# A mixed mLSTM and attention block: both groups of transposes directly behind each block of scores

## The chip, the cores and the metric

The kernel runs on one core of a Trainium2 chip. The metric is the device time of one execution in microseconds (us). Of the kernel before there are three timed runs (median 1693.31 us) and one execution under the hardware profiler.

## What is computed

One layer with two branches over a sequence of 1024 tokens and a width of 1024, all in float32. Cut to what matters here:

```
h = rmsnorm(x)
proj = h @ w_in                       # 12 segments: q, k, v, o, z, gates of branch a; q, k, v, z of branch b; two gates
branch a: mLSTM in both directions over 4 heads of 256 (chunked recurrence), rmsnorm, times sigmoid(o) * silu(z)
branch b: for each of 8 heads of 128:
    dq, dk = rope(q), rope(k)                            # two halves j of 64
    p = softmax(dq_0 dk_0 / 8) - lam * softmax(dq_1 dk_1 / 8)
    y_b = rmsnorm(p @ v) * silu(z)
mix = sigmoid(g_a) * (y_a @ w_branch_a) + sigmoid(g_b) * (y_b @ w_branch_b)
out = rmsnorm(x + mix @ w_out)
```

## The kernel before

Each product in float32 is made of three matmuls on halves: an operand is split into a high part H (rounded) and a low part L (the rest), and HH + HL + LH is summed in PSUM. Names that end in H and L are these parts.

The program runs in stages: an opening and a stage of projections with fewer products (to about 480 us), the attention (branch b, to about 1140 us), the mLSTM (branch a, to about 1400 us), then the mixing and the output. `build` writes down **units**, small pieces of work of TensorE with all that other engines do for them, in one list. On TensorE the order of that list is kept; on VectorE (DVE), ScalarE (ACT) and GpSimd (POOL) the framework's scheduler sets an order of its own, fixed at build time, and each engine takes its instructions strictly in that order. SyncE (SP) issues the DMAs.

In the attention the list is made by a planner, `Weaver`. It keeps a clock of its own, and `weave` merges the attention's own units with filling work (projections for the next head, products with v's weights, gate projections): it always takes the unit that is ready first. When a unit is ready follows from the table `LAG` (how long after another unit, and how long a PSUM bank is held) and from the number of banks.

The units of a head h, with t the block of 128 queries:
- S (`scores`): 12 matmuls on 64 rows each into two tiles S of 128x1024, which take four of the eight PSUM banks. VectorE finds the maximum (nm, L1066), ScalarE the exponential (e, L1068), VectorE the weighted difference of both (L1074).
- T (`transposes`), two groups of four transposes of e. Each group takes one of the two T banks; ScalarE copies it to pH (L1087), VectorE makes pL (L1088), and then the bank is free.
- PV (`pv`): 24 products with v for two blocks, in one T bank; ScalarE copies the result to att (L1101).
- M (`squares`): two transposes of att in a T bank, which ScalarE squares and sums (L1111). After the last pair GpSimd makes the scale rs from it (rb_v, rb_y, L146 to L152, L1118).
- G (`scale`): four transposes of rs in a T bank; VectorE multiplies it into zg (L1131).

The filling work uses the other two banks, pj. `da_proj` makes q and k of the next head: two projections (L552, "rope weights"), which VectorE multiplies by cos and sin (m, hl, L984 to L996); GpSimd rotates and splits them in six operations (L997 to L1001), and eight DMAs bring them to kst and qq (L1006). The tile hl exists once. `da_v` makes v for two heads (L574; ScalarE vH, VectorE vL L1043). `fill(n)` takes n gate projections; the tuple `FILL` says how many each head gets.

The mLSTM begins with loads of keys, values and gate rows (k, v, gb, HL in `ml_units`). Its keys are transposed and weighted (kwH by ScalarE, L1216), while W is made of gb by GpSimd (L1271) and ScalarE (L1273).

Of the kernel before, what the change touches and what calls it, by code (L numbers as in the profile page):

```python
# [8 lines left out]
F32R = mybir.dt.float32r  # L9
# [5 lines left out]
S = 1024  # L15
# [13 lines left out]
def two_pi_parts():  # L29
# [5 lines left out]


INF = 1.0e9
FILL = (0, 0, 0, 0, 0, 0, 0, 1)
Z_EARLY = (0, 1, 3, 5)
MM = 0.214  # L40
TP = 0.109

LAG = dict(Th=2.2, Sh=5.0, PVh=3.7, Mh=8.1, qk=14.0, T=6.8, PV=3.7, M=4.5, F=6.0, TTh=1.9, TT=3.2, POh=1.6,
           PO=1.7, Wh=0.3, W=2.0, STh=2.1, ST=4.9, th=1.8, t=4.1, aq=9.0, outh=6.6, out=14.0, G=6.0)


class Unit:
# [5 lines left out]
    def __init__(self, cost, fn, keys=(), tag=None, hold=0.0, name=None, after=(), lane=0):  # L53
        self.cost, self.fn, self.keys = cost, fn, keys
        self.tag, self.hold, self.name, self.after, self.lane = tag, hold, name, after, lane


def wide(t):

    return t.rearrange("p k e -> p (k e)").rearrange("p (k e) -> p k e", e=256)  # L60


class Weaver:
# [2 lines left out]
    def __init__(self):  # L66
        self.now, self.free, self.ends, self.banks, self.out, self.coming = 0.0, {}, {}, {}, [], set()

    def ready(self, u):
        t = 0.0  # L70
        for n, d in u.after:
            t = max(t, self.ends.get(n, INF if n in self.coming else 0.0) + d)
        if u.tag:
            held = sorted(self.free.get(u.tag, []))
            n = self.banks.get(u.tag, 1)
            if len(held) >= n:
                t = max(t, held[-n])
        return t

    def put(self, u):  # L80
        self.now = max(self.now, self.ready(u)) + u.cost
        if u.tag:
            self.free[u.tag] = (self.free.get(u.tag, []) + [self.now + u.hold])[-8:]
        if u.name:
            self.ends[u.name] = self.now
        self.out.append(u)
# [5 lines left out]
    def weave(self, *lists):  # L92


        lanes = {}
        for i, un in enumerate(lists):
            total, c = sum(u.cost for u in un) or 1.0, 0.0
            for u in un:
                lanes.setdefault((i, u.lane), []).append((c / total, u))
                c += u.cost  # L100
        self.coming = {u.name for un in lists for u in un if u.name}
        heads = list(lanes.values())
        while heads:
            best = min(heads, key=lambda l: (max(self.ready(l[0][1]), self.now), l[0][0]))
            u = best.pop(0)[1]
            self.put(u)
            self.coming.discard(u.name)
            heads = [l for l in heads if l]


class Block:
# [862 lines left out]
    def da_proj(self, h, st):  # L974
        A, v, a, p, q = self.A, self.v, self.a, self.p, self.q
        w1 = self.w1
        fb = lambda x: x.bitcast(F32)
        kA, kB = ("rope", h, 0), ("rope", h, 1)

        def first(half, pa):  # L980
            c = slice(half * 512, (half + 1) * 512)
            m = [w1.tile([128, 512], F32, name=f"m{i}", tag=f"m{i}", bufs=1) for i in range(2)]
            st["m"] = m
            v.tensor_tensor(out=m[0], in0=pa, in1=self.cosT[:, c], op=ALU.mult)  # L984
            v.tensor_tensor(out=m[1], in0=pa, in1=self.sinT[:, c], op=ALU.mult)

        def second(half, pb):
            c = slice(half * 512, (half + 1) * 512)
            if half == 0:
                st["k"] = w1.tile([128, 2, S], F32R, name="kst", tag="kst", bufs=2)  # L990
            qq = st["q", half] = w1.tile([128, 2, 512], F32R, name="qq", tag="qq", bufs=3)
            m = st["m"]

            hl = w1.tile([128, 4, 512], F32R, name="hl", tag="hl", bufs=1)
            v.tensor_tensor(out=fb(hl[:, 2]), in0=pb, in1=self.sinT[:, c], op=ALU.mult)
            v.tensor_tensor(out=fb(hl[:, 3]), in0=pb, in1=self.cosT[:, c], op=ALU.mult)  # L996
            p.tensor_tensor(out=m[0], in0=m[0], in1=fb(hl[:, 2]), op=ALU.subtract)  # L997
            p.tensor_tensor(out=m[1], in0=fb(hl[:, 3]), in1=m[1], op=ALU.add)
            for i in range(2):
                p.tensor_copy(hl[:, i, :], m[i])  # L1000
                p.tensor_tensor(out=hl[:, 2 + i, :], in0=m[i], in1=fb(hl[:, i, :]), op=ALU.subtract)  # L1001
            for x in range(2):
                for i, to in enumerate((st["k"][:, :, c], qq)):
                    for j in range(2):
                        r, g = 64 * j + 32 * x, 64 * (1 - i) + 32 * j
                        q.dma_start(out=fb(to[r:r + 32]), in_=fb(hl[g:g + 32, x::2]))  # L1006

        kz = ("w_in", OFF["bz"] + 128 * h)

        def zz(half, ps):  # L1010
            st["g", half] = g = w1.tile([128, 512], F32, name="zg", tag="zg", bufs=2)
            a.activation(out=g, in_=ps, func=AF.Tanh, scale=0.5)
            v.scalar_tensor_tensor(out=g, in0=g, scalar=1.0, in1=ps, op0=ALU.add, op1=ALU.mult)

        qk = []
        for half in range(2):
            qk += self.proj(kA, half, lambda ps, half=half: first(half, ps))
            qk += self.proj(kB, half, lambda ps, half=half: second(half, ps), name=("qk", h))
        def load(half):
            t = w1.tile([128, 512], F32, name="zr", tag="zr", bufs=2)  # L1020
            q.dma_start(out=t, in_=self.zd[h][:, half * 512:(half + 1) * 512])
            zz(half, t)

        if h in Z_EARLY:
            z = [Unit(0.0, lambda half=half: load(half), name=("z", h) if half else None) for half in range(2)]
        else:
            z = self.proj(kz, 0, lambda ps: zz(0, ps)) + self.proj(kz, 1, lambda ps: zz(1, ps), name=("z", h))
        for half in range(2):
            z[(half + 1) * len(z) // 2 - 1].after = ((("G", h - 1, half), LAG["G"]),)
        return qk, z  # L1030

    def da_v(self, n, sts):

        a, v, w1 = self.a, self.v, self.w1

        def done(s2, ps):
            for i, st in enumerate(sts):
                if s2 == 0:
                    st["v"] = tuple(w1.tile([128, 8, 128], F32R, name=f"v{x}", tag=f"v{x}", bufs=3) for x in "HL")
                vH, vL = (x[:, 2 * s2:2 * s2 + 2, :] for x in st["v"])  # L1040
                src = ps[:, :, 128 * i:128 * i + 128]
                a.copy(vH, src)
                v.tensor_tensor(out=vL, in0=src, in1=vH.bitcast(F32), op=ALU.subtract)  # L1043
        return self.v_units("bv", n, done, ((("PV", 2 * n - 2, 3, 1), 0.0),))

    def da_parts(self, h, st):
        v, a, p, q, w1 = self.v, self.a, self.p, self.q, self.w1
# [76 lines left out]
        def scale(half):  # L1124
# [3 lines left out]
            for i in range(4):  # L1128
# [6 lines left out]
            S=lambda t: Unit(6 * MM, lambda: scores(t), tag="S", hold=LAG["Sh"], name=("S", h, t), after=((("qk", h), LAG["qk"]),)),  # L1135
            T=lambda t, g: Unit(4 * TP, lambda: transposes(t, g), tag="T", hold=LAG["Th"], name=("T", h, t, g),
                                after=((("S", h, t), LAG["T"]),)),
            PV=lambda t2, g: Unit(12 * TP, lambda: pv(t2, g), tag="T" if g == 0 else None, hold=LAG["PVh"], name=("PV", h, t2, g),
                                  after=((("T", h, 2 * t2 + 1, g), LAG["PV"]),)),
            M=lambda t2: Unit(2 * TP, lambda: squares(t2), tag="T", hold=LAG["Mh"], name=("M", h, t2),  # L1140
                              after=((("PV", h, t2, 1), LAG["M"]), (("z", h if t2 == 3 else -1), 0.0))),
            G=lambda half: Unit(4 * TP, lambda: scale(half), tag="T", hold=LAG["Th"], name=("G", h, half),
# [2 lines left out]
    @staticmethod  # L1145
    def da_cycle(cur, prev, t):

        before = cur if t > 0 else prev
        un = []
        if cur:  # L1150
            un.append(cur["S"](t))
        own = cur if t >= 4 else prev
        if own and t % 2 == 0:
            un.append(own["M"]((t // 2 - 2) % 4))
        if prev and t in (4, 5):
            un.append(prev["G"](t - 4))
        own = cur if t >= 3 else prev
        pair = ((t - 1) // 2 - 1) % 4
        if own and t % 2 == 1:
            un += [own["PV"](pair, 0), own["PV"](pair, 1)]  # L1160
        if before:
            un.append(before["T"]((t - 1) % 8, 0))
        if before:
            un.append(before["T"]((t - 1) % 8, 1))
        return un


# [206 lines left out]
    def ml_units(self, heads, gates):  # L1374
# [4 lines left out]
        x, un = heads[0], []  # L1379
        take = lambda n: [gates.pop(0) for _ in range(n)]  # L1380
        hl = lambda x, c: x["gb"](c) + x["HL"](c)
        un += x["k"](3) + x["gb"](0) + x["v"](3) + x["k"](2) + x["v"](2) + x["k"](1) + x["HL"](0) + x["v"](1)
        un += take(8) + x["weigh"](3, 1) + take(3) + x["state"](3, 1) + x["k"](0) + x["v"](0)
        un += x["weigh"](2, 1) + take(5) + x["state"](2, 1) + hl(x, 1)
        un += x["weigh"](1, 1) + take(4) + x["state"](1, 1) + x["split"](0)
# [177 lines left out]
    def build(self):  # L1563
# [21 lines left out]
        with pool(name="const", bufs=1) as self.const, \  # L1585
# [99 lines left out]
            w.banks.update(S=1, T=2)  # L1685
            qk, z = zip(*[self.da_proj(h, sts[h]) for h in range(NH_B)])
            v0 = self.da_v(0, sts[0:2])
            w.add(do(lambda: setattr(self, "ahead", True)), *fill(1), *qk[0], *z[0], *v0[:20])
            prev = None
            for h in range(NH_B):  # L1690
                cur = self.da_parts(h, sts[h])
# [90 lines left out]
```

## Time and profile before

| | us |
|---|---|
| three runs | 1692.19, 1693.31, 1695.94 |
| the profiled execution | 1692.5 |
| its span, first to last instruction | 1690.7 |
| TensorE busy | 1640.5 |
| VectorE busy | 1019.6 |
| ScalarE busy | 774.9 |
| GpSimd busy | 660.4 |
| mean granted clock of TensorE | 0.995 |

The profiled execution lies 0.8 us under the median of the runs. In the lines below, PE is TensorE's matmuls and PEld its weight loads. "L552" is a line of the kernel, "pj<-hH,wH" says what is written from what, and "[2.15 <-DVE hl L996]" that the engine stood idle for 2.15 us, until VectorE's instruction of line 996 was done. Matmuls overlap, so on TensorE the distance from start to start tells what one costs, not its duration. A row of the waits reads: who waited, for whom, us in total, times, the longest.

### The profile page before, as it was taken

The page shows a single profiled execution, that of the slowest core. Times are in us where ns is not written, and L with a number is a line of the kernel's source. Part 1 is how long each engine was busy: PE and PEld are TensorE (multiplying, and loading weights), DVE is VectorE, ACT ScalarE, POOL GpSimd, SP SyncE. Part 2 cuts the span into 40 slices and gives each one's busy share as a digit, 9 for nine tenths or more (in the row PEclk, how much of TensorE's full clock was granted, in tenths as well). Part 3 has the DMA queues.
Part 4 walks back from the last instruction along what each step waited for, and adds up shares of the span by engine and source line. Part 5 has one row for each costly group of instructions (what it writes and reads, how often), then busy time and mean ns, then how long its engine had stood idle before and what let it go on. Part 6 is the DMA issues. An engine that isn't in the chain of part 4 may idle for free. (4 is left out here: it accounts for less than half of the span.)

```text
span 1690.7 us, 25288 instructions
## 1 busy us (share of the span) xinstructions
PE 1640.5 (97%) x9335; PEld 1377.7 (81%) x9335; DVE 1019.6 (60%) x1817; ACT 774.9 (46%) x1548; POOL 660.4 (39%) x713
## 2 busy tenths in 40 slices
PE   7999999999999999999999999999999999999998
PEld 5898778878778779788887977788988877888887
DVE  5634876787743876777676677713666664245533
ACT  6433555555532545544544555524566654022221
POOL 5754676666644343425154343222232222212000
PEclk9999999999999999999999999999999999999999
DMA  5433434443443132223132122028877527443222
GB/s 180 148 125 127 140 113 143 120 137 112 125 149 88 51 75 68 53 68 88 38 88 51 44 76 63 32 88 270 264 203 216 165 82 273 145 167 100 75 94 81
DMA packets 189710, 199.75 MB, mean 118 GB/s; under 512 B 11929, under 2 KB 143346, under 8 KB 189586
## 3 DMA queue, kind: packets, MB, share of 16 engines
q1 hardware_dynamic: 188386, 196.03, 38.3%
q10 hardware_dynamic: 1200, 2.11, 0.3%
q8 instruction: 73, 1.20, 0.3%
q14 instruction: 51, 0.42, 0.1%
HBM read 124.60 MB, written 56.72 MB: 107 GB/s over the span
## 5 line engine op out<-in xcount | busy, mean ns | idle before, releaser
L552 PE MATMUL pj<-hH,wH 128*128 128x512 f32 x640 | 267.7, 418 | 1.9 <-ACT f L665 1.5
L552 PE MATMUL pj<-hH,wL 128*128 128x512 f32 x640 | 252.4, 394 | 1.7 <-POOL wL L210 1.7
L552 PE MATMUL pj<-hL,wH 128*128 128x512 f32 x640 | 251.5, 393 | 0.2 <-DVE hL L703 0.2
L1068 ACT ACTIVATE e<-S,nm 128x1024 f32<-128x1024 f32 x128 | 142.6, 1115 | 98.2 <-DVE nm L1066 97.6
L212 POOL TENSOR_TENSOR wL<-raw,wH 128x1024 fp32r<-128x1024 f32 x34 | 83.6, 2458 | 216.3 <-ACT wH L207 208.3
L1066 DVE TENSOR_REDUCE nm<-S 128x1 f32<-128x1024 f32 x128 | 150.6, 1219 | 21.6 <-PE S L1063 21.0
L552 PEld LDWEIGHTS pj<-hH,wH 128*128 128x128 f32 x640 | 121.6, 190 | 32.7 <-issue 12.0
L552 PEld LDWEIGHTS pj<-hH,wL 128*128 128x128 f32 x640 | 120.7, 189 | 30.9 <-POOL wL L210 3.7
L552 PEld LDWEIGHTS pj<-hL,wH 128*128 128x128 f32 x640 | 121.4, 190 | 18.1 <-DVE hL L703 0.6
L1088 DVE TENSOR_TENSOR pL<-T,pH 128x512 fp32r<-128x512 f32 x128 | 87.1, 687 | 64.9 <-ACT pH L1087 63.7
L552 PE MATMUL pj<-sl_yb,wH 128*128 128x512 f32 x384 | 118.8, 390 | 2.6 <-DVE sl_yb L1449 2.1
L1087 ACT CAST pH<-T 128x512 fp32r<-128x512 f32 x128 | 75.0, 587 | 80.6 <-PE T L132 79.2
L1063 PE MATMUL S<-kst,qq 64*128 64x512 f32 x768 | 107.2, 408 | 0.4 <-ACT e L1068 0.4
L207 ACT CAST wH<-raw 128x1024 fp32r<-128x1024 f32 x48 | 50.5, 1052 | 122.0 <-PE pj L552 103.6
L1074 DVE SCALAR_TENSOR_TENSOR e<-e,r,e 128x1024 f32<-128x1024 f32 x64 | 93.1, 1455 | 2.2
L349 PE MATMUL T<-TH,wH 128*128 128x512 f32 x256 | 87.0, 399 | 2.6 <-ACT u L356 2.6
L1063 PEld LDWEIGHTS S<-kst,qq 64*128 64x128 f32 x768 | 68.3, 184 | 25.9 <-issue 11.8
L552 PEld LDWEIGHTS pj<-sl_yb,wH 128*128 128x128 f32 x384 | 72.1, 188 | 18.6 <-DVE sl_yb L1449 2.8
L349 PE MATMUL T<-TH,wL 128*128 128x512 f32 x256 | 86.1, 397 | 1.1 <-ACT u L356 1.1
L496 DVE SCALAR_TENSOR_TENSOR pj<-cin,cols,pj 128x512 f32<-128x512 f32 x128 | 87.0, 748 | 0.0
L132 PE MATMUL T<-ident,e 128*128 128x128 f32 x512 | 76.9, 273 | 7.9 <-ACT att L1101 4.1
L574 PE MATMUL pj<-wH,hH 128*128 128x256 f32 x256 | 76.1, 297 | 2.2 <-DVE hl L996 2.2
(398 smaller groups left out, 4400.0 us busy)
## 6 DMA issues: line engine op xcount, KB each, us to landing
raw<-in_w_in_dram SPq DMA_DIRECT2D x84, 512.0 KB, 3.8
kst<-hl SPq DMA_DIRECT2D x64, 128.0 KB, 2.4
qq<-hl SPq DMA_DIRECT2D x64, 128.0 KB, 2.4
x<-in_x_dram SPq DMA_DIRECT2D x8, 512.0 KB, 6.6
avH<-tz SPq DMA_DIRECT2D x16, 256.0 KB, 2.0
cak<-y SPq DMA_DIRECT2D x16, 256.0 KB, 2.9
cakH<-cin SPq DMA_DIRECT2D x16, 256.0 KB, 4.5
cakL<-tz SPq DMA_DIRECT2D x16, 256.0 KB, 4.6
```

The source lines that it names most:

```text
L132: self.t.transpose(out, in_, self.ident[0:k, 0:k])
L212: self.p.tensor_tensor(out=wL, in0=raw, in1=wHf, op=ALU.subtract)
L349: self.t.matmul(ps, lhsT=l[:, k, :], rhs=r[:, k, :], start=(first and k == 0 and m == 0), stop=(k == 3 and m == 2), skip_group_check=not f ...
L496: v.scalar_tensor_tensor(out=acc, in0=raw[:, o + x:o + x + 512], scalar=w(x), in1=acc, op0=ALU.mult, op1=ALU.add)
L552: self.t.matmul(ps, lhsT=l[:, k, :], rhs=r, start=(n == 0), stop=(n == 23))
L574: self.t.matmul(ps[:, i, :], lhsT=l, rhs=r[:, k, :], start=(kh == 0 and k == 0 and m == 0), stop=(kh == 1 and k == 3 and m == 2))
L1063: self.t.matmul(ps[:, o], lhsT=qq[r, x, c], rhs=k[r, y, o], start=(m == 0), stop=(m == 2))
L1066: v.tensor_reduce(out=nm, in_=ps, axis=AX.X, op=ALU.max, negate=True)
L1068: a.activation(out=e, in_=ps, func=AF.Exp, bias=nm[:, 0:1], accum_out=Z[:, j, t:t + 1])
L1074: v.scalar_tensor_tensor(out=e0, in0=e, scalar=r[:, 0:1], in1=e0, op0=ALU.mult, op1=ALU.add)
L1087: a.copy(pH[:, :, s], ps)
L1088: v.tensor_tensor(out=pL[:, :, s], in0=ps, in1=pH[:, :, s].bitcast(F32), op=ALU.subtract)
```

## The change

In the attention, the planner gets a `Chain`: several units that are placed as one, ready only when each part can run in its turn. `da_cycle` now chains the scores of block t with both groups of transposes of block t-1. Squares and products with v change places between even and odd t, and come earlier; the transposes of rs stand at t = 2 and 4 instead of 4 and 5. Some numbers of `LAG` follow. Beside this, hl has two places, products with v wait in the plan for a unit named "v", one gate fill (48 projections) moves from the attention's entry to its last head, and the first loads of the mLSTM are in another order.

```diff
-FILL = (0, 0, 0, 0, 0, 0, 0, 1)
+FILL = (0, 0, 0, 0, 0, 0, 0, 2)
-LAG = dict(Th=2.2, Sh=5.0, PVh=3.7, Mh=8.1, qk=14.0, T=6.8, PV=3.7, M=4.5, F=6.0, TTh=1.9, TT=3.2, POh=1.6,
+LAG = dict(Th=2.9, Sh=5.0, PVh=2.9, Mh=2.0, qk=14.0, T=6.8, PV=3.0, M=1.5, F=6.0, TTh=1.9, TT=3.2, POh=1.6,
...
+class Chain:
+    def __init__(self, *parts):
+        self.parts, self.cost, self.lane, self.name = parts, sum(u.cost for u in parts), 0, parts[0].name
...
-    def ready(self, u):
+    def ready(self, u, taken=0):
         t = 0.0
+        if isinstance(u, Chain):
+            c, used = 0.0, {}
+            for x in u.parts:
+                t = max(t, self.ready(x, used.get(x.tag, 0)) - c)
+                c += x.cost
+                used[x.tag] = used.get(x.tag, 0) + 1
+            return t
...
-            hl = w1.tile([128, 4, 512], F32R, name="hl", tag="hl", bufs=1)
+            hl = w1.tile([128, 4, 512], F32R, name="hl", tag="hl", bufs=2)
...
     def da_cycle(cur, prev, t):
         before = cur if t > 0 else prev
-        un = []
-        if cur:
-            un.append(cur["S"](t))
-        own = cur if t >= 4 else prev
+        un = [cur["S"](t)] if cur else []
+        if before:
+            un += [before["T"]((t - 1) % 8, g) for g in range(2)]
+        un = [Chain(*un)] if len(un) > 1 else un
+        if prev and t in (2, 4):
+            un.append(prev["G"](t // 2 - 1))
+        own = cur if t >= 2 else prev
+        pair = (t // 2 - 1) % 4
         if own and t % 2 == 0:
-            un.append(own["M"]((t // 2 - 2) % 4))
-        if prev and t in (4, 5):
-            un.append(prev["G"](t - 4))
-        own = cur if t >= 3 else prev
-        pair = ((t - 1) // 2 - 1) % 4
+            un += [own["PV"](pair, g) for g in range(2)]
         if own and t % 2 == 1:
-            un += [own["PV"](pair, 0), own["PV"](pair, 1)]
-        if before:
-            un.append(before["T"]((t - 1) % 8, 0))
-        if before:
-            un.append(before["T"]((t - 1) % 8, 1))
+            own = cur if t >= 3 else prev
+            un.append(own["M"](pair))
         return un
...
-        un += x["k"](3) + x["gb"](0) + x["v"](3) + x["k"](2) + x["v"](2) + x["k"](1) + x["HL"](0) + x["v"](1)
+        un += x["k"](3) + x["v"](3) + x["k"](2) + x["v"](2) + x["k"](1) + x["v"](1) + hl(x, 0)
...
-            w.add(do(lambda: setattr(self, "ahead", True)), *fill(1), *qk[0], *z[0], *v0[:20])
+            w.add(do(lambda: setattr(self, "ahead", True)), *qk[0], *z[0], *v0[:20])
```

The lines of the changed kernel carry higher numbers (L552 is L570, L1063 is L1083, L1066 is L1086, L132 is L150). What the change does to the engines' orders is shown at three places.

**TensorE in the attention, around one block of scores** (third head). Before, from the last group of transposes ahead of the scores on; e is the block's probabilities, pj a projection of the filling work, att the squares' input:

```order
L132 MATMUL T<-ident,e_6865 128x128 x4
L1063 MATMUL S<-kst,qq 128x512 x12
L552 MATMUL pj<-hH_187,wH 128x512
L552 MATMUL pj<-hL_189,wH 128x512
L552 MATMUL pj<-hH_187,wL 128x512
L132 MATMUL T<-ident,att 128x128 x2
```

and now:

```order
L570 MATMUL pj<-hH_186,wL 128x512
L1083 MATMUL S<-kst,qq 128x512 x12
L150 MATMUL T<-ident,e_6939 128x128 x8
L570 MATMUL pj<-hH_187,wH 128x512
L570 MATMUL pj<-hL_189,wH 128x512
```

The two groups of transposes, which had projections between them and stood ahead of the scores or anywhere in the block, now are eight in a row behind the scores. Of 64 blocks of scores, 10 were followed by transposes; now 63 are, and nine to fifteen projections (or up to 30 products for v) follow them, in most blocks twelve.

**VectorE at the attention's entry**, from the first half's hl to the first block of scores. Before:

```order
L995 TENSOR_TENSOR hl<-pj,sinT 128x512
L996 TENSOR_TENSOR hl<-pj,cosT 128x512
L984 TENSOR_TENSOR m_4719<-pj,cosT 128x512
L985 TENSOR_TENSOR m_4720<-pj,sinT 128x512
L1043 TENSOR_TENSOR vL<-pj,vH 128x256
L995 TENSOR_TENSOR hl<-pj,sinT 128x512
L996 TENSOR_TENSOR hl<-pj,cosT 128x512
L1043 TENSOR_TENSOR vL<-pj,vH 128x256 x3
L1066 TENSOR_REDUCE nm<-S 128x1 x2
```

and now:

```order
L1013 TENSOR_TENSOR hl<-pj,sinT 128x512
L1014 TENSOR_TENSOR hl<-pj,cosT 128x512
L1002 TENSOR_TENSOR m_4657<-pj,cosT 128x512
L1003 TENSOR_TENSOR m_4658<-pj,sinT 128x512
L1013 TENSOR_TENSOR hl<-pj,sinT 128x512
L1014 TENSOR_TENSOR hl<-pj,cosT 128x512
L1061 TENSOR_TENSOR vL<-pj,vH 128x256 x4
L1086 TENSOR_REDUCE nm<-S 128x1 x2
```

The second half's hl stood behind the first vL, and now stands ahead of it.

**ScalarE at the mLSTM's entry**; gt is a gate's output, kn a copy of transposed keys. Before:

```order
L1273 ACTIVATE W_11561<-W_11561,gc_negM 128x128
L1273 ACTIVATE W_11567<-W_11567,gc_negM 128x256
L960 ACTIVATE gt<-pj,gbh 128x512
L1216 ACTIVATE kwH<-T,gc_ws 128x256
L1273 ACTIVATE W_11610<-W_11610,gc_negM 128x256
L1273 ACTIVATE W_11616<-W_11616,gc_negM 128x128
L1216 ACTIVATE kwH<-T,gc_ws 128x256
```

and now:

```order
L978 ACTIVATE gt<-pj,gbh 128x512 x2
L1233 ACTIVATE kwH<-T,gc_ws 128x256 x2
L1230 COPY kn<-T 128x512
L1233 ACTIVATE kwH<-T,gc_ws 128x256
L1290 ACTIVATE W_11561<-W_11561,gc_negM 128x128
L1233 ACTIVATE kwH<-T,gc_ws 128x256
```

The first chunk's kwH stood behind W, and now stands ahead of every W; the second chunk's second kwH is behind one. On GpSimd, in the second head alone, five of rope's six operations (L1016, L1018, L1019) now stand between those that make rs.

More of the change, by code (lines that the diff above doesn't have):

```diff
@@ L74, in ready @@
             held = sorted(self.free.get(u.tag, []))
-            n = self.banks.get(u.tag, 1)
+            n = self.banks.get(u.tag, 1) - taken
             if len(held) >= n:
@@ L80, in put @@
     def put(self, u):
+        if isinstance(u, Chain):
+            self.now = max(self.now, self.ready(u))
+            for x in u.parts:
+                self.put(x)
+            return
         self.now = max(self.now, self.ready(u)) + u.cost
@@ L100, in weave @@
                 c += u.cost
-        self.coming = {u.name for un in lists for u in un if u.name}
+        self.coming = {x.name for un in lists for u in un for x in getattr(u, "parts", (u,)) if x.name}
         heads = list(lanes.values())
@@ L106, in weave @@
             self.put(u)
-            self.coming.discard(u.name)
+            self.coming.difference_update(x.name for x in getattr(u, "parts", (u,)))
             heads = [l for l in heads if l]
@@ L1043, in done @@
                 v.tensor_tensor(out=vL, in0=src, in1=vH.bitcast(F32), op=ALU.subtract)
-        return self.v_units("bv", n, done, ((("PV", 2 * n - 2, 3, 1), 0.0),))
+        un = self.v_units("bv", n, done, ((("PV", 2 * n - 2, 3, 1), 0.0),))
+        un[-1].name = ("v", n)
+        return un
     def da_parts(self, h, st):
@@ L1138, in da_parts @@
             PV=lambda t2, g: Unit(12 * TP, lambda: pv(t2, g), tag="T" if g == 0 else None, hold=LAG["PVh"], name=("PV", h, t2, g),
-                                  after=((("T", h, 2 * t2 + 1, g), LAG["PV"]),)),
+                                  after=((("T", h, 2 * t2 + 1, g), LAG["PV"]), (("v", h // 2), 1.0))),
             M=lambda t2: Unit(2 * TP, lambda: squares(t2), tag="T", hold=LAG["Mh"], name=("M", h, t2),
```

## The prediction

> **What bounds the kernel now.** The page was read first, then the waits of TensorE, then busy time by stretch of the program, then TensorE's timeline.
>
> ```profile
> PE 1640.5 (97%) x9335; PEld 1377.7 (81%) x9335; DVE 1019.6 (60%) x1817; ACT 774.9 (46%) x1548; POOL 660.4 (39%) x713
> PEclk9999999999999999999999999999999999999999
> ```
>
> TensorE is the bound. The diff removes no matmul and adds none, so only three things can move the time: TensorE's waits, stretches in which its clock is low, and what a change of the kind of matmul costs. The waits between 480 and 1160 us, and the stretches (columns: us, then busy time of PE, PEld, DVE, ACT, POOL with counts, granted clock, DMA share, GB/s):
>
> ```profile
> PE T L132 <- ACT att L1101: 4.1, 5, 1.8
> PE T L132 <- ACT T L1111: 2.6, 4, 1.2
> PE T L128 <- ACT kwH L1216: 2.4, 1, 2.4
> PE pj L574 <- DVE hl L996: 2.2, 1, 2.2
> ```
>
> ```profile
> 520.70:524.00 3.30, 3.30 (x16) 3.30 (x17) 0.20 (x1) 0.00 (x0) 3.23 (x4) 0.52 0.00 0
> 532.00:1146.00 614.00, 604.85 (x3906) 503.64 (x3906) 415.86 (x562) 303.19 (x637) 230.69 (x240) 1.00 0.24 63
> 1053.00:1104.00 51.00, 47.68 (x299) 37.68 (x298) 38.03 (x49) 28.81 (x62) 12.48 (x14) 1.00 0.12 37
> 1149.30:1155.40 6.10, 6.10 (x21) 5.41 (x22) 2.21 (x5) 2.21 (x6) 0.00 (x0) 0.50 1.07 382
> ```
>
> The attention (532 to 1146) has 614.00 - 604.85 = 9.15 us of idle TensorE; 51.00 - 47.68 = 3.3 of it stand in the last head. 4.1 + 2.6 = 6.7 of the 9.15 are transposes that wait until ScalarE has read a T bank (L1101, L1111). Ahead of the attention stands one wait of 2.2 us, behind it one of 2.4, and after each the granted clock is half for some us. That is all there is to win, with one thing that no wait shows: the switches.
>
> ```profile
> 563.10 1.65 PE L1063 MATMUL S<-kst,qq 64*128 64x512 f32 x12
> 564.69 0.44 PE L132 MATMUL T<-ident,att 128*128 128x128 f32 x2
> 564.88 0.48 PE L552 MATMUL pj<-hH,wH 128*128 128x512 f32 x1
> ```
>
> ```profile
> 856.62 1.66 PE L1063 MATMUL S<-kst,qq 64*128 64x512 f32 x12
> 858.21 0.51 PE L552 MATMUL pj<-hH,wH 128*128 128x512 f32 x1
> 858.55 0.39 PE L552 MATMUL pj<-hL,wH 128*128 128x512 f32 x1
> 858.78 0.39 PE L552 MATMUL pj<-hH,wL 128*128 128x512 f32 x1
> 859.01 0.38 PE L132 MATMUL T<-ident,att 128*128 128x128 f32 x2
> 859.15 0.48 PE L552 MATMUL pj<-hH,wH 128*128 128x512 f32 x1
> ```
>
> Starts are read here, since the durations overlap. A block of scores holds TensorE 1.59 us, whatever follows. The first projection behind it takes 858.55 - 858.21 = 0.34 against 0.23 of the next: 0.11 lost. Two transposes behind it take 564.88 - 564.69 = 0.19 against 859.15 - 859.01 = 0.14 elsewhere: 0.05 lost. So transposes stand there 0.06 us cheaper.
>
> **The change, part by part.**
>
> *Switches.* In the order of before, 54 of the 64 blocks of scores are followed by projections or products with v, 10 by transposes; in the changed order 63 are followed by the eight transposes of the block ahead. Blocks keep their count. Gain: 54 x 0.06 = 3.2 us. The row used is the transpose of att behind scores, the nearest to the new pair; as a bound, no gain if the first transpose of e costs what a projection does. [...]
>
> *Second place for rotated q, k (hl).* This is the wait ahead of the attention:
>
> ```profile
> 518.91 0.42 DVE L1043 TENSOR_TENSOR vL<-pj,vH 128x256 fp32r<-128x256 f32 x1 [9.10 <-ACT vH L1042]
> 519.28 0.69 DVE L995 TENSOR_TENSOR hl<-pj,sinT 128x512 f32<-128x512 f32 x1
> ```
>
> ```profile
> 520.62 0.44 PE L574 MATMUL pj<-wH,hH 128*128 128x256 f32 x1 [2.15 <-DVE hl L996]
> ```
>
> On VectorE the second half's hl stands behind a vL that TensorE feeds only at 518; the products with v then wait for the pj bank that hl has yet to read. In the changed order hl stands ahead of all vL, so the 2.2 us go, and with them the half clock behind: (1 - 0.52) x 3.3 = 1.6. Gain 3.8.
>
> *The gate fill moved from the entry to the last head.* 48 projections at 0.23 us, the same work. What they covered at the entry are the rope weights:
>
> ```profile
> 472.15 2.52 POOL L197 TENSOR_TENSOR wL<-raw,wH 128x512 fp32r<-128x512 f32 x2 [1.17 <-PE T L349]
> ```
>
> The first pair is ready at 474.7, before projections begin at about 480, and in the changed order it stands one place earlier on GpSimd. The next cover is between the second half's rotation and the first scores: six operations of GpSimd, then eight DMAs.
>
> ```profile
> 502.70 1.30 POOL L997 TENSOR_TENSOR m<-m,hl 128x512 f32<-128x512 f32 x1 [8.37 <-DVE hl L995]
> ...
> 507.80 1.28 POOL L1001 TENSOR_TENSOR hl<-m,hl 128x512 fp32r<-128x512 f32 x1
> ```
>
> ```profile
> 511.26 1.24 SPq L1006 DMA_DIRECT2D qq<-hl  x2
> ```
>
> ```profile
> qq<-hl SPq DMA_DIRECT2D x64, 128.0 KB, 2.4
> ```
>
> From 502.70 to the last issue's end at 512.5, plus 2.4 to landing, is 12.2 us; 132 products with v, at 0.12 each (half the columns of a projection at 0.23), cover 15.8. Cost 0; if the cover were short, the first scores would wait for qq. In the last head the fill covers the 3.3 us counted above.
>
> *New order in the attention.* Which waits does it make? Walk through one block from the first transpose behind the scores (time 0), with
>
> ```profile
> L1068 ACT ACTIVATE e<-S,nm 128x1024 f32<-128x1024 f32 x128 | 142.6, 1115 | 98.2 <-DVE nm L1066 97.6
> ...
> L1066 DVE TENSOR_REDUCE nm<-S 128x1 f32<-128x1024 f32 x128 | 150.6, 1219 | 21.6 <-PE S L1063 21.0
> ...
> L1088 DVE TENSOR_TENSOR pL<-T,pH 128x512 fp32r<-128x512 f32 x128 | 87.1, 687 | 64.9 <-ACT pH L1087 63.7
> ...
> L1087 ACT CAST pH<-T 128x512 fp32r<-128x512 f32 x128 | 75.0, 587 | 80.6 <-PE T L132 79.2
> ...
> L1074 DVE SCALAR_TENSOR_TENSOR e<-e,r,e 128x1024 f32<-128x1024 f32 x64 | 93.1, 1455 | 2.2
> ```
>
> ```profile
> 858.32 1.22 DVE L1066 TENSOR_REDUCE nm<-S 128x1 f32<-128x1024 f32 x1 [0.23 <-PE S L1063]
> ```
>
> ```profile
> 542.32 1.04 PE L132 MATMUL T<-ident,e 128*128 128x128 f32 x8
> ```
>
> VectorE begins 858.32 - 858.21 = 0.1 behind the scores and runs two reduces (to 2.5), then pL twice: the first T bank is free at 3.2, the second at 3.9. TensorE has eight transposes (0.9, since the next matmul starts before the 1.04 of the row are over) and twelve projections (2.8), and asks for a T bank at 3.7: 0.5 us to spare. ScalarE copies pH twice (to 1.9) and then takes both exponentials (to about 4.2); the weighted sum of both, 1.5 us, ends near 6.2, and the shortest block (1.6 + 0.9 + 2.8 + 0.1 for two transposes + 2.1 for nine projections = 7.5) asks for it later. So in a common block nothing waits, and the 9.1 us go. Where it does: five blocks have nine projections there (T bank asked for at 3.0; 0.25 each, 1.2 in all); once, at the end of the first head, squares follow the chain at once (3.2 - 0.9 = 2.3). The third place is the head's scale rs, which now follows the last squares by one block instead of two:
>
> ```profile
> 1127.26 0.23 POOL L146 TENSOR_SCALAR rb_v<-ms 128x8 f32<-128x8 f32 x1 [6.85 <-ACT T L1111]
> ...
> 1130.73 0.23 POOL L1118 TENSOR_SCALAR rb_y<-rb_y 128x8 f32<-128x8 f32 x1
> ```
>
> Squares are read by ScalarE at about 5.2, and this chain takes 3.7: 8.9, while the transposes of rs come at 7.5 + 3.7 = 11.2. That has room, except in the second head, where the changed order of GpSimd puts rope's operations between those of rs: rb_v begins behind the first of them (5.9), and five of the six (5.1 us) lie in between, so 5.9 + 3.7 + 5.1 = 14.7, a wait of 3.4. New waits 1.2 + 2.3 + 3.4 = 6.9. Bounds: 0, if rs and the first head fall out better, and without limit above; the rival below prices that.
>
> *Loads of the mLSTM's first head.*
>
> ```profile
> 1140.79 0.43 SPq L1188 DMA_DIRECT2D gb<-gg  x1
> ...
> 1141.92 0.61 SPq L1196 DMA_DIRECT2D vL<-avL  x1
> ```
>
> ```profile
> 1147.05 1.24 POOL L1271 TENSOR_SCALAR_AFFINE_SELECT W<-gb 128x128 f32<-128x128 f32 x4 [3.76 <-DMA gb<-gg]
> ```
>
> ```profile
> 1149.27 0.55 PE L128 MATMUL T<-vH,kwH 128*128 128x258 f32 x1 [2.40 <-ACT kwH L1216]
> ```
>
> On ScalarE the weighted keys kwH stand behind W, which hangs on the gates' load gb. TensorE waits 2.4 us, and then has (1 - 0.50) x 6.1 = 3.0 of half clock. In the changed order kwH stands ahead of every W, and gb is loaded behind all k and v. v's load starts 0.5 earlier, lands near TensorE's arrival, and I leave 0.5 of wait. The second chunk's last kwH is still behind one W, whose gb now is issued some 5 us later (behind eight loads; the rows are 0.57 apart and more): 1.0 of wait. Gain 5.4 - 1.5 = 3.9; bounds 0 and 5.4. The clock stays up, as both rests are far below the two waits that pulled it down. [...]
>
> **Sum.** 3.2 + 3.8 + 9.1 - 6.9 + 3.9 = 13.1 us. The profiled execution took 1692.5 (its span 1690.7 and 1.8 around), 0.8 below the median of 1693.3 of the three runs; from that median 1680.2.
>
> **Rivals.**
> - *Clean* (faster still): no new wait at all. 3.2 + 3.8 + 9.1 + 5.4 = 21.5, so 1672. For it: the walk leaves room nearly everywhere. Against: three places where it does not.
> - *Entry and mLSTM keep their waits elsewhere*: 7.7 us less gain, 1688. For it: a load moved back is late for someone. Against: both causes are gone from the engine's order.
> - *The two T banks* (slower). Now both are taken at once, and whoever wants one next has 0.5 us. Where VectorE or ScalarE come late to reduce or pH, by two operations of rope (1.4) or one cast of weights, TensorE waits 0.9. Over 62 chains a mean wait of 13.1 / 62 = 0.21 eats the gain; 0.9 in half of them is 28 us, less the 13.1: 1708. For it: VectorE is at 415.86 of 614. Against: in the changed order reduce and pL stand together on VectorE, and what it does ahead has the 1.6 us of scores to end. Its milder form (0.15 to 0.25 in the mean) gives no change, 1690 to 1696.
> - *The clock falls behind the chains.* 63 falls of 1.6 each would be 101 us: 1781. Against it: eight transposes together at 542.32, and clock 1.00 from 532 to 1146. [...]
>
> **Chances.** Forecast 0.60 (1675 to 1686 by itself), clean 0.13, other waits 0.11, T banks mild 0.09, T banks in full 0.06, clock 0.01. Faster by over 0.2% (3.4 us, about what this measurement tells from no change): 0.84; within 0.2%: 0.09; slower: 0.07. The range 1670 to 1690 leaves out the banks in both forms, the clock, and the edge of clean. Of round numbers I take 1680.
>
> **What would show it.** Right: TensorE's waits on L1101 and L1111 (numbered anew) gone from the table, idle in the attention under 7 us; no wait on hl and no clock below 1.00 near 508 and near 1140; rs waited for once, in the second head. Wrong: many short waits of transposes or products with v for pL in every block; or a fall of the clock in the attention, or a wait at the first scores for qq.

## The result, and the profile after

The changed kernel takes 1683.09 us (median of four runs, 1682.54 to 1685.78) against 1693.31: ratio 0.9941, interval 0.9923 to 0.9958. The forecast was 1680, between 1670 and 1690, faster. The total fell into the range; how it is shared out among the edits did not come out, as the experiments show. Two executions are left out of all that follows: one of 7635 us of a kernel further down, and one of 2684 us of the kernel before.

The profiled execution after is the slowest of the four: 1685.78, its span 1684.0. Its page, first the busy times, then the granted clock in 40 slices:

```profile
PE 1637.8 (97%) x9335; PEld 1375.7 (82%) x9335; DVE 1023.6 (61%) x1817; ACT 766.7 (46%) x1548; POOL 669.0 (40%) x713
...
PEclk9999999999999999999999999999999999999999
```

The waits of TensorE between the first scores (518.1) and the first product of the mLSTM (1139.2), all of them (us, times, longest):

```profile
PE T L150 <- POOL rb_y L1138: 3.4, 1, 3.4
PE T L150 <- DVE pL L1108: 2.0, 1, 2.0
PE T L1119 <- DVE pL L1108: 1.4, 4, 0.5
PE T L150 <- DVE e L1094: 0.9, 1, 0.9
```

The waits on att and on squares (L1121, L1131 now) are gone, the wait on hl ahead of the scores too. In their place stand the rs of the second head (rb_y), the end of the first head (pL, once), four short waits of products with v, and one for e. By stretch, the same columns as before; the first row is the attention, the second its last head and end, the third the first products of the mLSTM:

```profile
518.12:1139.20 621.08, 613.17 (x3954) 510.99 (x3954) 420.74 (x564) 299.62 (x644) 242.76 (x242) 1.00 0.25 66
...
1050.00:1139.20 89.20, 89.20 (x499) 73.56 (x498) 36.42 (x49) 36.31 (x74) 22.41 (x35) 1.00 0.27 83
1139.20:1156.00 16.80, 14.79 (x84) 12.66 (x83) 5.76 (x12) 6.39 (x13) 4.64 (x12) 1.00 0.96 302
```

Idle in the attention: 621.08 - 613.17 = 7.9 us, all of it ahead of the last head, which has none. What the two kernels take from one marker to the next, by the starts of the same matmuls on TensorE (markers: the first projection behind the rope weights, the first scores, the first product of the weighted keys, the first scores of the mLSTM; the 48 projections of the moved fill, 10.88 us at 0.2267, are taken out of the stretch they stand in):

| us | before | after | gain | forecast |
|---|---|---|---|---|
| opening, unchanged code | 481.05 | 481.57 | -0.5 | 0 |
| entry, to the first scores | 40.45 | 36.55 | 3.9 | 3.8 |
| attention (before without its 2.4 of kwH) | 614.5 | 610.2 | 4.3 | 5.4 |
| kwH wait and first products of the mLSTM | 19.9 | 16.8 | 3.1 | 3.9 |
| all behind, unchanged code | 524.0 | 527.9 | -4.0 | 0 |
| span | 1690.7 | 1684.0 | 6.7 | 13.1 |

The three changed stretches give 11.2 of the 13.1. The unchanged code behind took 4.0 back in this execution. Up to TensorE's last matmul 6.8 us of it ran at half clock (granted 0.50 from 1415.84 to 1422.66), against 3.4 before (1398.03 to 1401.44), which is 1.7 of the 4.0; another 1.9 are longer waits for sl_yb, the parts of y_b (2.9 and 1.6 us on VectorE's and ScalarE's, against 2.1 and 0.5). The last section shows which waits had half clock behind them. Between the medians the gain is 10.2.

### The profile page after: what moved, and what is told of

Read it like the earlier page. It is cut to its first block, busy times and chain, and to the rows that moved or that the text cites. A ratio compares the mean times of both kernels' runs of the same rounds, so it can differ in the third digit from the quotient of the medians.

```text
span 1684.0 us, 25335 instructions
## 1 busy us (share of the span) xinstructions
PE 1637.8 (97%) x9335; PEld 1375.7 (82%) x9335; DVE 1023.6 (61%) x1817; ACT 766.7 (46%) x1548; POOL 669.0 (40%) x713
## 5 line engine op out<-in xcount | busy, mean ns | idle before, releaser
L570 PE MATMUL pj<-hH,wH 128*128 128x512 f32 x640 | 261.9, 409 | 1.5 <-ACT f L683 1.5
L570 PE MATMUL pj<-hH,wL 128*128 128x512 f32 x640 | 252.5, 395 | 1.3 <-POOL wL L228 1.3
L570 PE MATMUL pj<-hL,wH 128*128 128x512 f32 x640 | 251.6, 393 | 0.0
L1086 DVE TENSOR_REDUCE nm<-S 128x1 f32<-128x1024 f32 x128 | 150.7, 1219 | 110.7 <-PE S L1083 110.7
L1107 ACT CAST pH<-T 128x512 fp32r<-128x512 f32 x128 | 68.8, 589 | 169.9 <-PE T L150 169.9
L570 PEld LDWEIGHTS pj<-hH,wL 128*128 128x128 f32 x640 | 121.0, 189 | 29.5 <-POOL wL L228 3.1
L570 PEld LDWEIGHTS pj<-hH,wH 128*128 128x128 f32 x640 | 121.7, 190 | 20.8 <-ACT f L683 1.8
L570 PEld LDWEIGHTS pj<-hL,wH 128*128 128x128 f32 x640 | 121.2, 189 | 19.5 <-DVE hL L721 0.3
L570 PE MATMUL pj<-sl_yb,wH 128*128 128x512 f32 x384 | 121.2, 396 | 4.5 <-DVE sl_yb L1466 2.9
L1083 PE MATMUL S<-kst,qq 64*128 64x512 f32 x768 | 106.1, 408 | 0.0
L1094 DVE SCALAR_TENSOR_TENSOR e<-e,r,e 128x1024 f32<-128x1024 f32 x64 | 101.5, 1587 | 1.8
L1083 PEld LDWEIGHTS S<-kst,qq 64*128 64x128 f32 x768 | 67.4, 184 | 29.8 <-issue 9.7
L570 PEld LDWEIGHTS pj<-sl_yb,wH 128*128 128x128 f32 x384 | 73.3, 191 | 21.6 <-DVE sl_yb L1466 3.8
L1108 DVE TENSOR_TENSOR pL<-T,pH 128x512 fp32r<-128x512 f32 x128 | 82.0, 682 | 5.9 <-ACT pH L1107 5.9
L215 POOL TENSOR_TENSOR wL<-raw,wH 128x512 fp32r<-128x512 f32 x32 | 51.1, 1609 | 67.7 <-ACT wH L214 62.5
L570 PE MATMUL pj<-sl_yb,wL 128*128 128x512 f32 x192 | 75.7, 394 | 0.0
```

Of the source, the lines that this page charges most:

```text
L215: self.p.tensor_tensor(out=vw(wL), in0=src, in1=vw(wHf), op=ALU.subtract)
L570: self.t.matmul(ps, lhsT=l[:, k, :], rhs=r, start=(n == 0), stop=(n == 23))
L1083: self.t.matmul(ps[:, o], lhsT=qq[r, x, c], rhs=k[r, y, o], start=(m == 0), stop=(m == 2))
L1086: v.tensor_reduce(out=nm, in_=ps, axis=AX.X, op=ALU.max, negate=True)
L1094: v.scalar_tensor_tensor(out=e0, in0=e, scalar=r[:, 0:1], in1=e0, op0=ALU.mult, op1=ALU.add)
L1107: a.copy(pH[:, :, s], ps)
```

## The experiments

Ten kernels in eleven runs, each against the kernel before. Ratios are to before, with 95% intervals; "above" and "below" compare medians with the changed kernel's 1683.09. The changed kernel was timed in one group only, above; the kernel before, timed again with each group of experiments, had medians of 1692.06 to 1692.97 instead of 1693.31. So differences of about 1 us to the changed kernel say nothing.

**Each part undone alone.** Two places for hl back to one (first), the old order of loads (second), the 48 projections back to the entry (third), the old order and due times of the attention (fourth):

```
-hl = w1.tile([128, 4, 512], F32R, name="hl", tag="hl", bufs=2)
+hl = w1.tile([128, 4, 512], F32R, name="hl", tag="hl", bufs=1)
```

> The changed kernel with one place for rotated q, k (hl) instead of two, all else as changed. Theory (the prediction's): the second half's hl stands behind vL again, TensorE waits 2.2 us for it ahead of the first scores and runs about 3.4 us at half clock behind it; about 3.9 us slower than the changed kernel (1687 against 1683). Rival: the wait went because the fill moved or because products with v come in another order; then no wait on hl, 0 us.

1686.11 us, ratio 0.9962 (0.9948 to 0.9976), 3.0 above the changed kernel. Its table of TensorE's waits has the old one back, at its old size:

```profile
PE pj L592 <- DVE hl L1014: 2.2, 1, 2.2
```

The entry takes 38.96 us instead of 36.55: 2.4, and no half clock behind it (granted 1.00, rows in the last section). So the wait belongs to hl (theory), but its 1.6 of half clock does not always come: before, 40.45.

```
-un += x["k"](3) + x["v"](3) + x["k"](2) + x["v"](2) + x["k"](1) + x["v"](1) + hl(x, 0)
+un += x["k"](3) + x["gb"](0) + x["v"](3) + x["k"](2) + x["v"](2) + x["k"](1) + x["HL"](0) + x["v"](1)
```

> The changed kernel with the old order of loads ahead of the mLSTM (gates' row first, v of the second direction last). Theory: the weighted keys wait for W before the first product as they did (2.4 us and half a clock for 6.8 us), so 5.8 us of loss against the 2.2 us wait that the changed kernel still has at its second chunk: about 3.1 us slower, 1686. Rival: the loads' order only moves the wait, 0 us.

1688.52 us, ratio 0.9975 (0.9961 to 0.9989), 5.4 above. The longest wait for kwH in its table is 2.9 us, at the first product:

```profile
PE T L146 <- ACT kwH L1233: 3.5, 4, 2.9
```

From the first scores to the mLSTM's the trace has 640.7 against 637.9, a loss of 2.7. The profiled execution is the fastest of the seven (1685.89), so it doesn't show where the rest of the 5.4 lies. The theory's cause holds; its price is 2.7 by the trace, and up to 5.4 by the medians.

```
-FILL = (0, 0, 0, 0, 0, 0, 0, 2)
+FILL = (0, 0, 0, 0, 0, 0, 0, 1)
-w.add(do(lambda: setattr(self, "ahead", True)), *qk[0], *z[0], *v0[:20])
+w.add(do(lambda: setattr(self, "ahead", True)), *fill(1), *qk[0], *z[0], *v0[:20])
```

> The changed kernel with the 48 gate projections back at the entry to the attention, so that the last head has one fill less. Theory: the entry is the same (0), but the last head ends without cover: its last squares follow the last chain at once, as in the first head, and wait 2.0 to 2.3 us for a T bank with about 1.6 us of half clock behind, and the transposes of e wait some 3 us in all: 3 to 6 us slower, 1686 to 1689. Rival (cost 0 either way, the cover isn't needed): 0 us.

1690.44 us (median of ten executions), ratio 0.9988 (0.9977 to 0.9998). 7.4 above the changed kernel, more than expected (the next text's 7.7 is by the median of all eleven). It was run once more for a profile:

> The kernel with the 48 gate projections back at the entry once more, for a profile. It took 7.7 us more than the changed kernel. Theory: the waits stand in the last head, for e, for a T bank behind the last chain, each with half a clock; first scores at the same time as in the changed kernel but for the 10.9 us of the 48 projections. Rival: the entry loses something (a wait ahead of the first scores).

1689.62 us. The entry takes 47.43 - 10.88 = 36.55 us, to the hundredth what it takes without the fill: cost 0 there is shown. The attention takes 8.5 us more. Its waits in the attention, to be read against the four rows of the kernel after:

```profile
PE T L150 <- DVE pL L1108: 4.7, 3, 2.0
PE T L150 <- POOL rb_y L1138: 3.5, 1, 3.5
PE T L1119 <- DVE pL L1108: 3.0, 4, 2.3
PE T L150 <- DVE e L1094: 1.1, 2, 0.8
```

4.6 us more of waiting, and a mean granted clock of 0.99 over the attention instead of 1.00. The added waits stand in the last head, 5.0 us between 1053 us and the attention's end, where the changed kernel has none:

```profile
PE T L150 <- DVE pL L1108: 2.7, 2, 2.0
PE T L1119 <- DVE pL L1108: 2.3, 1, 2.3
```

Without the moved fill the new order is 4.2 us slower than the old in these two executions (618.7 against 614.5, both with the one fill that the last head had before).

```
-            un += [before["T"]((t - 1) % 8, g) for g in range(2)]
-        un = [Chain(*un)] if len(un) > 1 else un
...
+            un.append(before["T"]((t - 1) % 8, 0))
```

> The changed kernel with the attention's old order (transposes spread between other work, old due times); hl, the mLSTM's loads and the fill stay changed. Theory: the waits on att and squares return (9.1 us, less about 3 that the fill in the last head now covers) and the switches cost 3 again, while the changed order's own waits go (7.9 us and 1.6 of half clock): within 1 us of the changed kernel, so the new order as it stands is worth almost nothing. Rival (the prediction's sum for the order alone, 9.1 + 3.2 - 6.9): 5.4 us slower, 1688.

1681.82 us, ratio 0.9936 (0.9922 to 0.9951): 1.3 *below* the changed kernel's 1683.09, inside the intervals. The new order as it stands is worth nothing that these runs can tell; the rival, 5.4 us slower, falls. In the traces its attention takes 620.3 us, against 621.1. In its table of waits those on att and squares stand again, but the fill has cut them from 6.7 to 5.5:

```profile
PE T L150 <- ACT att L1121: 4.2, 5, 1.8
...
PE T L150 <- ACT T L1131: 1.3, 3, 0.5
```

**The fill alone**: the two lines of its move, on the kernel before.

> The kernel before with the move of the 48 gate projections alone. Theory: they cover the last head's waits (3.3 us) and uncover nothing at the entry: 1688 to 1689 against 1692. Rival 1: the move is worth what taking it back cost, nearly 8 us: 1684. Rival 2: cost and gain 0, 1692.

1687.09 us, ratio 0.9966 (0.9955 to 0.9977): 5.9 faster, by the smallest edit of the four. Between the two expectations: more than the 3.3 of idle time that the last head showed. In its trace the entry is 1.5 shorter with the same 2.2 us on hl (no half clock behind it this time: the products with v then start 0.12 us apart, where before they started 0.21 apart at 0.50). The attention takes 620.12 - 10.88 = 609.2 instead of 614.5, and its idle time falls from 614.49 - 605.34 = 9.2 to 620.12 - 614.77 = 5.4. The stretch in the kernel before, then in this one:

```profile
532.38:1146.87 614.49, 605.34 (x3906) 503.77 (x3905) 415.86 (x562) 303.19 (x637) 230.69 (x240) 1.00 0.24 64
```

```profile
520.08:1140.20 620.12, 614.77 (x3954) 512.32 (x3953) 415.38 (x562) 305.17 (x640) 233.94 (x241) 1.00 0.24 65
```

**The switch measured by itself.** One more 128x512 matmul in every block, once behind the scores and once ahead of them:

```
 ps = self.bank("T", (128, 4, 128))
+if g == 0:
+    self.t.matmul(ps.rearrange("p a b -> p (a b)"), lhsT=self.hH[0][:, 0, 0:128], rhs=self.hH[0][:, 0, :], start=True, stop=True)
```

```
+self.t.matmul(both[0][:, 0:512], lhsT=self.hH[0][:, 0, 0:128], rhs=self.hH[0][:, 0, :], start=True, stop=True)
 for o in (slice(0, 512), slice(512, S)):
```

> The changed kernel with one additional 128x512 matmul (its result is overwritten) between each block of scores and the first transposes, 64 in all. Theory (what follows the scores decides what the switch costs): each costs 0.227 plus the 0.055 by which a projection behind scores is dearer than a transpose: 64 x 0.282 = 18.0 us above the changed kernel, and 3.5 above the same matmul put ahead of the scores. Rival (the switch costs the same whatever follows): 14.5, and no difference to the other place.

> The changed kernel with the same additional 128x512 matmul ahead of each block of scores (its result is overwritten by them), 64 in all. Both theories: 64 x 0.227 = 14.5 us above the changed kernel, less up to 3 where the added work covers waits for a T bank. It is the measure for the one with the matmul behind the scores: theory 3.5 us faster than that, rival equal.

Ahead of the scores: 1697.67 us (ratio 1.0030, 1.0014 to 1.0045), 14.6 above the changed kernel; 14.5 was expected. Behind them: 1754.42 (1.0359, 1.0336 to 1.0382), 71.3 above. Neither theory has the 71.3, so the total does not decide; the block's starts do. TensorE's timeline in the kernel after, and in the one with the matmul behind the scores (start, us, operation):

```profile
664.54 1.66 PE L1083 MATMUL S<-kst,qq 64*128 64x512 f32 x12
666.13 1.09 PE L150 MATMUL T<-ident,e 128*128 128x128 f32 x8
666.98 0.48 PE L570 MATMUL pj<-hH,wH 128*128 128x512 f32 x1
```

```profile
1015.92 1.66 PE L1083 MATMUL S<-kst,qq 64*128 64x512 f32 x12
1017.51 0.50 PE L1106 MATMUL T<-hH 128*128 128x512 f32 x1
1017.86 1.03 PE L150 MATMUL T<-ident,e 128*128 128x128 f32 x8
1018.65 0.48 PE L570 MATMUL pj<-hH,wH 128*128 128x512 f32 x1
```

From the scores to the projection: 2.44 us, and 2.73. Over all 63 chains the median from the start of the last matmul of the scores to the start of the second transpose is 0.489 against 0.770: 0.281 for a matmul that takes 0.227 elsewhere. So 0.054 of it is the switch, and what follows the scores decides its size here: in the kernel before, the first matmul behind scores took 0.111 us extra as a projection (0.338 instead of 0.227) and 0.056 as a transpose of att (0.165 instead of 0.109); in the kernel after, the first transpose of e took 0.165 too.

Most of the other 53 us are the prediction's slow rival, the two T banks, as this kernel's waits and its VectorE timeline show:

```profile
PE T L1121 <- DVE pL L1110: 40.8, 29, 3.4
```

```profile
1021.56 0.69 DVE L1110 TENSOR_TENSOR pL<-T,pH 128x512 fp32r<-128x512 f32 x1 [1.59 <-ACT pH L1109]
...
1024.27 1.28 DVE L1094 SCALAR_TENSOR_TENSOR e<-e,r,e 128x1024 f32<-128x1024 f32 x1
1025.47 0.68 DVE L1110 TENSOR_TENSOR pL<-T,pH 128x512 fp32r<-128x512 f32 x1
```

VectorE's order came out another way there: the second pL stands behind the weighted sum of e, which waits for both exponentials. In 29 blocks the products with v wait for it, up to 3.4 us, and the mean granted clock of the execution is 0.988, against 0.993 in the kernel after. The mechanism is real; in the changed kernel the two pL follow each other, and it costs 1.4 in four places.

**A mended version.** First try: one fill into the first head, rs one block later, and the gates' row (gb) loaded earlier.

```
-FILL = (0, 0, 0, 0, 0, 0, 0, 2)
+FILL = (1, 0, 0, 0, 0, 0, 0, 2)
-        if prev and t in (2, 4):
+        if prev and t in (3, 5):
-un += x["k"](3) + x["v"](3) + x["k"](2) + x["v"](2) + x["k"](1) + x["v"](1) + hl(x, 0)
+un += x["k"](3) + x["v"](3) + x["gb"](0) + x["k"](2) + x["v"](2) + x["k"](1) + x["v"](1) + x["HL"](0)
```

> The changed kernel with its three remaining waits taken on: one fill of 48 gate projections (from those behind the mLSTM) goes into the first head, the transposes of rs stand one block later in every head, and the first gates' row is loaded ahead of the second k. Theory: the waits on pL at the first head's end (2.0 us and 1.7 of half clock), on rs in the second head (3.4) and on kwH behind W (2.2) go: 7.6 to 9.3 us less than the changed kernel, about 1675. Rival: they come back elsewhere (the yb loads behind the mLSTM lose the cover of 48 projections, the first products of the mLSTM wait for loads pushed back by the gates' row): within 3 us of the changed kernel.

1689.7 us, ratio 0.9983 (0.9972 to 0.9994), 6.6 above the changed kernel: the waits came back elsewhere, as the rival had it, and cost more than its 3 us. The fill taken from behind the mLSTM left too little there. (That list is so short now that one piece of three matmuls is run and summed twice, in the last gate projection, so this kernel's result is off; only its time and waits are read here.) And the earlier gb put a pair of W ahead of the first chunk's second kwH on ScalarE. Its waits:

```profile
PE T L146 <- ACT kwH L1233: 5.2, 4, 4.6
PE pj L570 <- DVE sl_yb L1466: 4.7, 5, 1.8
PE pj L570 <- ACT sl_yb L1465: 3.8, 5, 2.0
```

The second try moves no work out of its place, and loads gb later instead of earlier:

```
-        if prev and t in (2, 4):
+        if prev and t in (3, 5):
...
-                main = sum((self.da_cycle(cur, prev, t) for t in range(8)), [])
+                main = tail + sum((self.da_cycle(cur, prev, t) for t in range(8)), [])
+                tail = [main.pop()] if h + 1 < NH_B else []
...
-        un += x["k"](3) + x["v"](3) + x["k"](2) + x["v"](2) + x["k"](1) + x["v"](1) + hl(x, 0)
-        un += take(8) + x["weigh"](3, 1) + take(3) + x["state"](3, 1) + x["k"](0) + x["v"](0)
+        un += x["k"](3) + x["v"](3) + x["k"](2) + x["v"](2) + x["k"](1) + x["v"](1) + x["HL"](0)
+        un += take(8) + x["weigh"](3, 1) + take(3) + x["state"](3, 1) + x["k"](0) + x["v"](0) + x["gb"](0)
```

> The changed kernel with its three waits taken on in another way, no work moved out of place: the last squares of a head are planned with the next head's work, the transposes of rs stand one block later, and the first gates' row is loaded behind all k and v of the mLSTM's first head. Theory: pL at the first head's end (2.0 us, and 1.7 of half clock), rs (3.4) and kwH behind W (2.2) go: 7.6 to 9.3 us below the changed kernel's 1683, so 1674 to 1676. Rival: the new places are late for someone else again (W for the first chunk's products, z for the next head): above 1680.

The same lines for gb on the kernel with the attention's old order:

> The mended kernel with the attention's old order and due times (its waits on att and squares stay; the mLSTM's gates' row is late as in the mended one). Theory: 1682 of the changed kernel with the old order less 2.1 for kwH: about 1680, so 4 to 6 us slower than the mended one, of which 3.0 is the switches and the rest waits. Rival: the order of the attention makes no difference once the other waits are gone, equal to the mended one.

The mended kernel takes 1674.84 us, ratio 0.9890 (0.9876 to 0.9904): 8.3 below the changed kernel, as expected. With the attention's old order and the same loads it is 1678.29, ratio 0.9922 (0.9908 to 0.9935). The runs don't overlap (1669.79 to 1675.15, 1676.60 to 1681.13). So the new order is worth 3.5 us once its own waits are gone. In the two traces the difference lies in the attention, which is 7.9 us shorter in the mended kernel (613.4 against 621.3). All behind it is 6.5 longer there, 4.7 of it in code that is the same, so how much is the order's own stays open between 3.5 and 7.9. The attention of the mended kernel as a stretch, and all waits in it:

```profile
516.78:1130.19 613.41, 610.28 (x3954) 510.89 (x3954) 412.70 (x564) 301.68 (x644) 237.86 (x242) 1.00 0.25 66
```

```profile
PE T L1119 <- DVE pL L1108: 2.4, 5, 0.7
PE T L150 <- DVE e L1094: 0.7, 3, 0.4
```

Idle 3.1 us instead of 7.9, and nothing on rs or on the first head's end. Ahead of the mLSTM's first scores no wait on kwH is left in the table, but one of 1.0 us for which the profile names no cause (1141.42, just behind a kwH).

## Why the prediction was right, point by point

*Switches, 3.2.* Held. 54 blocks at 0.054 are 2.9; the row of the transpose of att was the right neighbour. The bound of no gain, a first transpose of e as dear as a projection, falls (0.056 us extra against 0.111).

*Second place for hl, 3.8.* The entry gained 3.9. Of this 2.4 is the wait and 1.5 the half clock, which was the luck of that one profile: two other kernels have the same wait (2.2 us) without it.

*Gate fill, 0 at the entry, 3.3 of cover.* The 0 is exact. The cover was mis-sized: alone the move brings 5.9, and taken back from the changed kernel it costs 7.4. The 3.3 was read off the last head in the old order; the new order, without the moved fill, waits 5.0 us there.

*Attention waits, 9.1 gone.* They are gone. The prediction gave the fill 3.3 of them and the order the other 5.8; measured, the fill alone takes 3.8 of idle time (9.2 to 5.4), and undoing the order brings 5.5 back. So the size held. What failed is the order's balance: 5.8 + 3.2 - 6.9 = 2.1 of gain by the prediction. By the traces 5.5 of waits and 2.9 of switches stand against 7.9 of new idle time and 1.7 of half clock, a loss of 1.2, and the kernel without the new order is 1.3 faster.

*New waits, 6.9.* 7.9 of idle time. The scale rs was forecast at 3.4 and took 3.4, for the cause given: GpSimd's timeline of the kernel after has five of rope's six operations between rb_v and the end of rb_y:

```profile
602.60 1.20 POOL L164 TENSOR_SCALAR rb_v<-ms 128x8 f32<-128x8 f32 x1
603.76 0.60 POOL L1018 CAST hl<-m 128x512 fp32r<-128x512 f32 x1
...
611.66 0.23 POOL L1138 TENSOR_SCALAR rb_y<-rb_y 128x8 f32<-128x8 f32 x1
```

The first head's end was forecast at 2.3 and took 2.0; the half clock behind it (1.7, rows below) was not forecast. The five blocks with nine projections, 1.2: four waits, 1.4. The 0.9 on e was missed.

*mLSTM loads, 3.9.* 3.1. The first chunk's 0.5 did not come; the second chunk's 1.0 was 2.0. It was sized by when gb would be issued (5 us later), not by how long it takes from there to W (1147.05 - 1140.79 = 6.3 us before). From the timelines of SP, GpSimd and TensorE after:

```profile
1138.34 0.60 SPq L1205 DMA_DIRECT2D gb<-gg  x1
```

```profile
1145.96 1.24 POOL L1288 TENSOR_SCALAR_AFFINE_SELECT W<-gb 128x128 f32<-128x128 f32 x4 [10.16 <-DMA gb<-gg]
```

```profile
1147.10 0.39 PE L146 MATMUL T<-vH,kwH 128*128 128x258 f32 x1 [1.99 <-ACT kwH L1233]
```

Here it is 7.6 us from issue to W, and kwH stands behind W on ScalarE. That the cause was still in the engine's order was written there; that gb could go behind all kwH instead was the mend.

*Rivals.* Clean is what the mended kernel comes near (1674.84; 1672 was given). The T banks did not strike here, and did in the kernel with one more matmul. A fall of the clock behind every chain did not come.

*The total.* By edit, the forecast was 3.8 for hl, 3.9 for the loads, 3.3 for the fill and 2.1 for the order. Measured were 3.0, 2.7 (up to 5.4), 5.9 by itself, and -1.3. That the total still fell so near is in part luck: the fill brought more than forecast and the order less.

*The signs.* The waits on att, on squares and on hl are gone, and rs was waited for once, in the second head, as named. But the attention's idle time is 7.9 us and not under 7, and the clock did fall once in the attention (to 0.50 at 579.57, for 3.41 us), which the prediction had named as a sign of being wrong.

## What to carry to other kernels

Undo each part alone before crediting a gain to the part that was meant to bring it: here the order of the attention, most of the diff, brought nothing until its own waits were mended (then 3.5 us), and moving 48 projections to the head that had no work left to fill its waits brought 5.9 by itself, of 10.2. A new order has to be walked to its ends, the last block of a stage and the first of the next, since its waits stood there, and the mend was to plan those few steps with the neighbour's work. A load is ready when it lands, not when it is issued (gb: 7.6 us to its use here, 6.3 before); and what stands behind its user in an engine's order (here kwH behind W on ScalarE) may be better served by a later load than by an earlier one.

## What the runs showed of the hardware

The granted clock was 0.50 behind TensorE's waits of 2.0, 2.15 and 2.40 us below, and stayed at 1.00 behind those of 1.99, 2.2 and 3.4. The first head's end, and the second head's longer wait, in stretches of the trace after (columns as above; the clock is the third from the end):

```profile
576.16:579.57 3.41, 1.39 (x9) 1.03 (x8) 3.03 (x6) 3.41 (x8) 3.41 (x5) 1.00 0.50 140
579.57:582.98 3.41, 3.41 (x10) 2.66 (x9) 1.72 (x2) 0.39 (x3) 3.24 (x4) 0.50 0.43 103
606.88:610.29 3.41, 1.62 (x8) 1.01 (x6) 2.89 (x7) 2.70 (x5) 3.41 (x4) 1.00 0.56 128
610.29:613.70 3.41, 1.75 (x15) 1.75 (x16) 1.06 (x2) 0.00 (x0) 3.00 (x7) 1.00 0.78 180
```

The wait of 2.0 us that ended at 578.46 (1.39 of 3.41 us busy) was followed by 3.41 us at 0.50, the wait of 3.4 us that ended at 611.95 (1.62 and 1.75 of 3.41 busy) by none. The wait on hl, 2.15 us in the kernel before and 2.2 with one place put back, was followed by 3.41 us at 0.50 in the first and by none in the second (the kernel before, then that one):

```profile
517.39:520.80 3.41, 1.26 (x10) 1.05 (x10) 1.89 (x4) 1.26 (x3) 0.75 (x1) 1.00 0.00 0
520.80:524.21 3.41, 3.41 (x17) 3.41 (x18) 0.10 (x1) 0.00 (x0) 3.35 (x4) 0.50 0.00 0
```

```profile
504.23:507.64 3.41, 1.82 (x16) 1.62 (x14) 1.15 (x3) 1.06 (x3) 0.00 (x1) 1.00 0.00 0
507.64:511.05 3.41, 2.84 (x23) 2.84 (x24) 0.85 (x2) 0.20 (x1) 3.35 (x4) 1.00 0.02 5
```

On kwH the wait of 2.40 us in the kernel before had a clock of 0.50 behind it for 6.1 us, the one of 1.99 in the kernel after had 1.00. So in these executions a wait of 2.0 to 3.4 us cost its length alone, or up to 1.7 more where 3.41 us at 0.50 followed (3.0 more for the 6.1), and the wait on hl came out both ways. The clock is a part of why the same code, from the mLSTM's first scores to the end, took 524.0 us in the trace before and 527.9 in the trace after: 1.7 of the difference is half clock, and 1.9 are longer waits for sl_yb. So gains under 2 us need many runs.
